# Ten weight splits of a decoder layer's first tile moved behind its softmaxes, and a separate buffer for one gate

## The chip, the cores and the metric

The kernel runs on one core of a Trainium2 chip. The metric is device time in microseconds (us) for one launch. The core's engines are named as in the profile: PE (TensorE matmuls; PEld is its weight load), DVE (VectorE), ACT (ScalarE), POOL (GpSimd) and SP (SyncE, which only issues DMAs here). Each engine works through its own list of instructions in order and waits on semaphores for the others.

## The reference, cut to what matters

One decoder layer over 2048 tokens of width 1024, in float32:

```python
h = rms_norm(x, pre_norm_g)
a_u, a_v, sq, sk, sv, mq, z = split(h @ w_in)          # 512 512 256 128 128 256 1024 columns
y_a = chunked_spatial_gating(gelu(a_u), gelu(a_v))      # chunks of 128 tokens, 4 groups
y_b = sliding_window_attention(sq, sk, sv)              # 4 heads, sinks, relative bias
mk, mv = split(rms_norm(mem, mem_norm_g) @ w_mem_kv)    # 256 memory tokens
y_c = memory_cross_attention(mq, mk, mv)                # 4 heads
y = concat(y_a, y_b, y_c) * silu(z)
x = x + rms_norm(y @ w_out, post_norm_g)
```

## The kernel before, in words

The tokens are worked on in four tiles of 512. For each tile the kernel forms the normalised input `hT` and multiplies it with 22 weight *units*, 128 x 1024 numbers each: four for the values of the spatial gating (`U_V`), then keys, values and queries, then the gate units `U_Z` (z) and the units `U_U` (u). The first tile also projects the memory (`gm`). After the four tiles a second part multiplies y with the output weights.

Precision comes from splitting: each operand is held as a high part (a rounded copy, made by ACT) and a low part (the difference, made by DVE or POOL), and each product is three matmuls: high with high, high with low, low with high. `split` (line 79) does this; the high copy is line 80 and the subtraction is line 81. So a unit is multiplied in 24 matmuls, and its third matmul is the first that reads the unit's low part. A row `whl<-wraw,whl` is the split of one unit from its raw load `wraw` into the pair `whl`.

A unit of the first tile is loaded raw and split once. The pair is then stored to DRAM (`split_d`), and later tiles load it from there. `weight_unit` (line 133) keeps a window: when unit number i of the order is due, units up to i+3 have been split and units up to i+4 are being loaded. There are three raw buffers and four buffers for pairs. Unit i+4's raw load goes into the buffer that held unit i+1's raw, so it waits, on SP, until unit i+1 has been split. SP issues nearly all other DMAs too, in program order: the stores of pairs, the stores `yd` of finished gates, the loads `xs` (for the next tile's sums of squares) and `xk` (the next tile's input).

In the second half of a tile, a counter of *slots* places attention work between the matmuls: one slot after each six matmuls of a unit, and one after each unit. In the first tile twelve softmaxes start in slots 14, 19, 24, 29 (the window attention, names `b_0` to `b_3`) and 33, 36 to 54 (the memory attention, `c_0_0` to `c_3_1`). Each has logits on PE (`l_b`, `l_c`), a maximum on DVE, exponentials on ACT and a normalisation on DVE; its transposes (`tp`) and its product with the values (`o`) follow on PE a fixed number of slots later. The last ten units of the first tile come in this order: U0, Z0, U1, Z1, Z6, Z7, U2, Z2, U3, Z3 (Z0 is `g_z_0` from `whl_10`, U0 is `g_u_0` from `whl_18`, and so on). A unit of kind U ends in a small product `sg` on PE and the tile `a` on DVE.

For later tiles there is a list `aside`: pieces of work put there are taken off one by one by `queue_aside` (line 399), which a softmax calls after its last exponential and its normalisation. They are issued behind these two, ACT work behind the exponential and DVE work behind the normalisation.

The order on PE and SP is the order in which the program is written. On ACT, DVE and POOL the framework's scheduler sets the order when the program is built, within the first part.

Near the end of each tile PE multiplies out `bc` (line 213), the next tile's scale: it needs `rsr_x` from POOL, which needs the sums of squares of eight loads `xs` (line 193 on ACT).

The gates of the window and memory outputs (`ZB`, four per tile, units Z4 to Z7) share two buffers under one tag, so the third gate is written where the first stood, and waits until that one's store to `yd` has landed. Tag `a` has three buffers.

Of the kernel before, what the change touches and what calls it, by code (L numbers as in the profile page):

```python
# [30 lines left out]
U_V, U_SV, U_K, U_Q, U_MQ, U_Z, U_U, U_O, U_MK, U_MV = 0, 4, 5, 6, 8, 10, 18, 22, 30, 32  # L31
# [2 lines left out]

W_OPS = ("B11", "B21", "B22", "T1", "T2", "T3", "T4")
STORE_AFTER = 6
TURN_SLOT = 30
A_SLOTS0, A_SLOTS = (14, 5, 8, 13, 33, 8, 13), (7, 5, 8, 13, 27, 7, 11)

# [2 lines left out]
def kernel(  # L42
# [32 lines left out]

    def f32(ap):
        return ap.bitcast(F32)

    def split(hi, lo, src, lo_engine=None):
        nc.scalar.copy(hi, src)  # L80
        (lo_engine or nc.vector).tensor_tensor(lo, src, f32(hi), ALU.subtract)  # L81
# [22 lines left out]
    made, stores = set(), []  # L104
# [4 lines left out]
    def load_unit(i):  # L109
        u, t = order[i]  # L110
        if u in wo_d or t > stored_at.get(u, 0):
            return
        raws[i] = raw_tile(f"wraw_{t}_{u}")
        for c in (slice(0, 512), slice(512, D)) if i == 0 else (slice(0, D),):
            nc.sync.dma_start(raws[i][:, c], wst[u][:, c])
            yield

    def split_unit(i):
        u, t = order[i]
        w = wp.tile([P, 2, D], F32R, tag="whl", name=f"whl_{t}_{u}")  # L120
        ready[u, t] = w
        if i not in raws:
            nc.sync.dma_start(f32(w), wo_d[u][t] if u in wo_d else split_d[u])
            return
        raw = raws.pop(i)
        for c in (slice(0, 512), slice(512, D)) if i == 0 else (slice(0, D),):
            split(w[:, 0, c], w[:, 1, c], raw[:, c], nc.vector if (i % 3 == 2 and i > 14) or i == 0 else nc.gpsimd)
        if stored_at.get(u) == t:
            stores.append((i, u, w))

    raws, loaded, halved = {}, [0], [0]

    def weight_unit(u, t):

        i = order.index((u, t))
        while halved[0] < min(i + 4, len(order)):
            if loaded[0] == halved[0]:
                list(load_unit(loaded[0]))
                loaded[0] += 1
            split_unit(halved[0])  # L140
            halved[0] += 1
        while loaded[0] < min(i + 5, len(order)):
            list(load_unit(loaded[0]))
            loaded[0] += 1

        while stores and stores[0][0] <= i:
            _, v, w = stores.pop(0)
            nc.sync.dma_start(split_d[v], f32(w))
        return ready.pop((u, t))

    def rms_rstd(ss, n, eps, name, tag=""):
# [86 lines left out]
    def group(w, t, tag, pool=None, slot=None, scaled=True):  # L238

        ps = (pool or ps_mm).tile([P, TS], F32, tag="t" if pool else "mm", name=f"g_{tag}")
        n = 0
        hT = hTs[t % 2]
        for k in range(KC):
            for wi, hi in ((0, 0), (0, 1), (1, 0)):
                nc.tensor.matmul(ps, w[:, wi, k * P : (k + 1) * P], hT[:, hi, k, :],  # L247
                                 start=(n == 0), stop=(n == 3 * KC - 1))
                n += 1
            if slot and k % 2 and k < KC - 1:  # L250
                slot(k // 2)
        if t == 0 and scaled:
            sc = sp.tile([P, TS], F32, tag="a", name=f"sc_{tag}", bufs=3)
            nc.vector.tensor_tensor(sc, ps, late["bcs"], ALU.mult)  # L254
            ps = sc
        return ps
# [87 lines left out]
    def project_memory(mT, slot):  # L344
        for u in range(4):
            w = weight_unit((U_MK if u < 2 else U_MV) + u % 2, 0)
            ps = ps_mm.tile([P, MEM], F32, tag="mm", name=f"gm_{u}")
            n = 0
            for k in range(KC):
                for wi, hi in ((0, 0), (0, 1), (1, 0)):  # L350
                    nc.tensor.matmul(ps, w[:, wi, k * P : (k + 1) * P], mT[:, hi, k, :],  # L351
                                     start=(n == 0), stop=(n == 3 * KC - 1))
                    n += 1
                if k % 4 == 3:
                    slot()
            if u == 3:
                turn_values(2)
            if u < 2:

                mks = sp.tile([P, MEM], F32, tag="e", name=f"mks_{u}", bufs=3)  # L360
                nc.vector.tensor_tensor(mks, ps, late["bcs_mem"], ALU.mult)
                for e in range(2):
                    h = 2 * u + e
                    src = mks[64 * e : 64 * e + 64, :]
                    split(MK[0:64, h, 0, :], MK[0:64, h, 1, :], src)
                    nc.scalar.copy(MK[64:128, h], f32(MK[0:64, h]))
            else:
                mvs = sp.tile([P, MEM], F32, tag="e", name=f"mvs_{u}", bufs=3)
                nc.scalar.copy(mvs, ps)
                late[u] = mvs  # L370

    def turn_values(u):

        tp = ps_mm.tile([P, 2, 2, 64], F32, tag="mm", name=f"mvt_{u}")
        for i in range(2):
            nc.tensor.transpose(tp[:, i].rearrange("p a b -> p (a b)"), late[u][:, i * P : (i + 1) * P], ident)
        hs = slice(2 * (u - 2), 2 * (u - 2) + 2)
        for i in range(2):
            r, hi = late["rstd_mem"][:, i : i + 1], MV[:, i, hs, 0, :]
            nc.scalar.mul(hi, tp[:, i], r)  # L380
            nc.vector.scalar_tensor_tensor(MV[:, i, hs, 1, :], tp[:, i], r, f32(hi), ALU.mult, ALU.subtract)
# [5 lines left out]
    def split_heads(ps, tag, shape_tag):  # L387
        S = sp.tile([P, 2, TS], F32R, tag=shape_tag, name=f"S_{tag}", bufs=1)
        for e in range(2):
            src = ps[64 * e : 64 * e + 64, :]  # L390
            nc.scalar.copy(S[0:64, e, :], src)
            nc.vector.tensor_tensor(S[64:128, e, :], src, f32(S[0:64, e, :]), ALU.subtract)
        return S


    aside = []

    def queue_aside(scalar, vector):
        with tc.issue_after(scalar.ins), tc.issue_after(vector.ins):
# [114 lines left out]
    def silu2(ps, tag, out_tag, bufs):  # L514

        G = sp.tile([P, TS], F32, tag=out_tag, name=f"Z_{tag}", bufs=bufs)
        nc.scalar.activation(G, ps, AF.Tanh, scale=0.5)
        nc.vector.scalar_tensor_tensor(G, G, 1.0, ps, ALU.add, ALU.mult)
        return G
# [3 lines left out]

    def store_later(dst, src, slots=STORE_AFTER):

        stores_due.append((tick[0] + slots, dst, src))
# [88 lines left out]
    for t in range(NT):  # L615
# [44 lines left out]
        for j in range(4):  # L660
# [3 lines left out]
            w = weight_unit(U_V + j, t)  # L664
# [78 lines left out]
        SB, SC, O, ZB = [split_heads(q0, f"q{t}_0", "S0")], [], {}, {}  # L743
# [33 lines left out]
        def slot(_=None):  # L777
            tick[0] += 1
            flush_stores()
            for job in jobs.pop(at[0], []):  # L780
                job()
            for stage, n in sorted(stages.pop(at[0], [])):
                if stage == 2:
                    running[n] = unit(n)
                next(running[n], None)
            if t == 0 and at[0] == TURN_SLOT:
                turn_values(3)
            at[0] += 1

        def slotted(u, tag, scaled=True):  # L790
            ps = group(weight_unit(u, t), t, tag, slot=slot, scaled=scaled)
            return ps
# [8 lines left out]
        def gate_bc(i):  # L801

            ps = slotted(U_Z + 4 + i, f"z{t}_{4 + i}")
            ZB[i] = silu2(ps, f"z{t}_{4 + i}", "ZB", 2)
            slot()

        def gate_a(g):
# [14 lines left out]
            slot()  # L822

        gate_bc(0)
        gate_bc(1)
        if t == 0:
            memory_along()
            project_memory(late["mT"], slot)
        gate_a(0)
        gate_a(1)  # L830
        gate_bc(2)
        gate_bc(3)
        gate_a(2)
# [18 lines left out]

    tick[0] += STORE_AFTER
    T2 = [weight_unit("T2", j) for j in range(2)]
# [327 lines left out]
```

## Time and profile before

| what | value |
|---|---|
| median of 3 runs | 785.67 us (781.81, 785.67, 788.67) |
| the profiled execution's own time | 783.76 us |
| its span, first to last instruction | 781.8 us |
| mean granted TensorE clock | 0.996 |
| busy: PE, PEld | 759.6 us, 638.2 us |
| busy: DVE, ACT, POOL | 567.6 us, 397.4 us, 157.8 us |

The span leaves out 2.0 us of the profiled execution that lie around it. PE is busy nearly all the time, so what a change of the other engines can do is read from the places where PE stands idle, not from the other engines' busy time.

### The profile page before, as it was taken

What the parts mean: (1) busy time and instruction counts of PE and PEld (TensorE: products, weight loads), DVE (VectorE), ACT (ScalarE), POOL (GpSimd) and SP (SyncE); (2) the same over time, 40 slices, a digit from 0 to 9 for tenths busy, and PEclk for the clock granted to TensorE, in tenths of its full rate; (3) what the DMA queues carried; (4) which work ended last, traced back from release to release, by engine and by line L of the source; (5) the groups of instructions that cost most, each with busy time, mean ns of one, the idle gap of its engine ahead of it and who ended that gap; (6) DMA issues with size and microseconds to landing.
All of it is one profiled execution on the core that took longest, in us unless ns stands there. A gap on an engine that the chain in (4) does not pass through costs nothing.

```text
span 781.8 us, 10715 instructions
## 1 busy us (share of the span) xinstructions
PE 759.6 (97%) x3788; PEld 638.2 (82%) x3788; DVE 567.6 (73%) x1052; ACT 397.4 (51%) x879; POOL 157.8 (20%) x141
## 2 busy tenths in 40 slices
PE   8999999899999999999999999999999999999994
PEld 7878987787888888888887788888888878888883
DVE  6497998795658789744796796748976325697787
ACT  7686666653654656355455553544434233343442
POOL 4565543220502210041031000201300000010013
PEclk9999999999999999999999999999999999999998
DMA  8856557736875996947989769864464699818717
GB/s 326 296 205 245 184 204 256 272 123 273 314 261 210 320 316 227 343 165 224 371 292 309 260 218 379 339 261 161 142 216 178 237 388 402 322 55 322 270 32 291
DMA packets 54133, 199.48 MB, mean 255 GB/s; under 512 B 5275, under 2 KB 5824, under 8 KB 43840
## 3 DMA queue, kind: packets, MB, share of 16 engines
q1 hardware_dynamic: 53552, 198.20, 70.1%
q8 instruction: 30, 0.49, 0.2%
q10 hardware_dynamic: 528, 0.59, 0.2%
q14 instruction: 23, 0.19, 0.1%
HBM read 142.15 MB, written 56.63 MB: 254 GB/s over the span
## 4 chain that ended last, share of the span: by engine, by line
PE 70%; DMA 13%; DVE 11%; ACT 3%; issue 2%; POOL 1%; SPq 0%; POOLq 0%; DVEq 0%; ACTq 0%
PE g_z L247 14%; PE v L674 9%; PE g_u L247 7%; PE Y_S L1030 6%; PE Y L1030 5%; PE g_q L247 4%; PE g_mq L247 4%; DMA xs<-in_x 4%; PE X L1030 3%; PE X_S L1030 3%; DMA yd<-Z_z 2%; DMA split_d<-whl 2%; PE g_sv L247 2%; PE g_k L247 2%; PE gm L351 1%
## 5 line engine op out<-in xcount | busy, mean ns | idle before, releaser
L247 PE MATMUL g_z<-hT,whl 128*128 128x512 f32 x768 | 193.7, 396 | 0.0
L247 PEld LDWEIGHTS g_z<-hT,whl 128*128 128x128 f32 x768 | 138.3, 188 | 25.0
L81 POOL TENSOR_TENSOR whl<-wraw,whl 128x1024 fp32r<-128x1024 f32 x30 | 73.6, 2456 | 139.8 <-ACT whl L80 92.8
L247 PE MATMUL g_u<-hT,whl 128*128 128x512 f32 x384 | 97.7, 396 | 0.0
L674 PE MATMUL v<-whl,hT 128*128 128x512 f32 x384 | 88.9, 391 | 2.2 <-DVE sc_z L254 1.7
L674 PEld LDWEIGHTS v<-whl,hT 128*128 128x128 f32 x384 | 71.6, 188 | 18.6 <-DVE sc_z L254 2.1
L247 PEld LDWEIGHTS g_u<-hT,whl 128*128 128x128 f32 x384 | 69.2, 188 | 12.7
L80 ACT CAST whl<-wraw 128x1024 fp32r<-128x1024 f32 (+1 forms) x39 | 40.0, 1027 | 25.5 <-DMA wraw<-in_wst 6.8
L928 POOL TENSOR_TENSOR r<-a,mhalf 128x1 f32<-128x1 f32 x16 | 13.7, 856 | 191.1 <-DVE a L926 178.2
L447 POOL TENSOR_SCALAR_AFFINE_SELECT pp_b<-po_b 128x512 fp32r<-128x512 f32 x30 | 19.9, 663 | 143.3 <-ACT po_b L80 143.3
L247 PE MATMUL g_q<-hT,whl 128*128 128x512 f32 x192 | 45.9, 394 | 0.0
L1030 PE MATMUL Y<-hT,yop 128*128 128x512 f32 x192 | 44.5, 391 | 0.8 <-DVE yop L903 0.8
L247 PE MATMUL g_mq<-hT,whl 128*128 128x512 f32 x192 | 44.7, 389 | 0.0
L1030 PE MATMUL Y_S<-hT,yop_S 128*128 128x512 f32 x192 | 44.2, 389 | 0.0
L1030 PEld LDWEIGHTS Y<-hT,yop 128*128 128x128 f32 x192 | 35.8, 188 | 9.2 <-DVE yop L903 1.7
L1030 PEld LDWEIGHTS Y_S<-hT,yop_S 128*128 128x128 f32 x192 | 36.0, 188 | 7.5
L247 PEld LDWEIGHTS g_q<-hT,whl 128*128 128x128 f32 x192 | 35.7, 188 | 7.8 <-issue 0.5
L247 PEld LDWEIGHTS g_mq<-hT,whl 128*128 128x128 f32 x192 | 35.9, 188 | 7.3
L483 ACT ACTIVATE L_c<-l_c,nm_c 128x256 f32<-128x256 f32 x48 | 22.3, 469 | 28.7 <-DVE nm_c L478 28.6
L432 ACT ACTIVATE Lc_b<-Lc_b,nm_b 128x129 f32<-128x129 f32 x64 | 25.1, 394 | 18.9 <-DVE nm_b L430 18.8
L157 POOL TENSOR_TENSOR rsr_v<-rsa_v,mhalf 128x4 f32<-128x4 f32 x16 | 17.4, 1090 | 82.0 <-DVE rsa_v L155 74.1
L704 ACT ACTIVATE vhat<-G_v,nb,rsr_v 128x128 f32<-128x128 f32 x64 | 26.4, 485 | 11.5 <-DVE nb L702 11.4
(209 smaller groups left out, 1477.2 us busy)
## 6 DMA issues: line engine op xcount, KB each, us to landing
whl<-split_d SPq DMA_DIRECT2D x54, 1024.0 KB, 6.3
split_d<-whl SPq DMA_DIRECT2D x22, 1024.0 KB, 8.3
wraw<-in_wst SPq DMA_DIRECT2D x37, 512.0 KB, 5.8
hT<-wo_B SPq DMA_DIRECT2D x10, 1024.0 KB, 9.3
wo_T<-hT SPq DMA_DIRECT2D x8, 1024.0 KB, 7.8
xr<-in_x SPq DMA_DIRECT2D x16, 512.0 KB, 8.6
y<-yd SPq DMA_DIRECT2D x7, 1024.0 KB, 13.2
xs<-in_x SPq DMA_DIRECT2D x24, 256.0 KB, 6.3
```

Of the source, the lines that this page charges most:

```text
L80: nc.scalar.copy(hi, src)
L81: (lo_engine or nc.vector).tensor_tensor(lo, src, f32(hi), ALU.subtract)
L157: nc.gpsimd.tensor_tensor(r, a, mhalf[:, :c], ALU.pow)
L247: nc.tensor.matmul(ps, w[:, wi, k * P : (k + 1) * P], hT[:, hi, k, :], start=(n == 0), stop=(n == 3 * KC - 1))
L351: nc.tensor.matmul(ps, w[:, wi, k * P : (k + 1) * P], mT[:, hi, k, :], start=(n == 0), stop=(n == 3 * KC - 1))
L432: last = nc.scalar.activation(Lc[:, h, : P + 1], Lc[:, h, : P + 1], AF.Exp, bias=nm[:, h : h + 1], accum_out=den[:, h : h + 1])
L447: nc.gpsimd.affine_select(prev[:, s], f32(own[:, s]), [[0, 4], [-1, P]], ALU.is_gt, 0.0, base=0, channel_multiplier=1)
L483: last = nc.scalar.activation(p[:, e, :], lg[:, e, :], AF.Exp, bias=nm[:, e : e + 1], scale=scale, accum_out=den[:, e : e + 1])
L674: nc.tensor.matmul(vps[i], hT[:, hi, 2 * j + kk, i * P : (i + 1) * P], w[:, wi, kk * 512 : (kk + 1) * 512], start=(j == 0 and (hi, wi, kk) ...
L704: nc.scalar.activation(vhat[:, i, g, :], G[:, g * P : (g + 1) * P], AF.Identity, bias=nb[:, g : g + 1], scale=rv[:, g : g + 1])
L928: nc.gpsimd.tensor_tensor(r, a, mhalf2[:, 0:1], ALU.pow)
L1030: nc.tensor.matmul(banks[m], a(s, k)[:, m * P : (m + 1) * P], w(v, k), start=first and n == 0, stop=n == 11, skip_group_check=not first)
```

## The change

For the first tile, the last ten units (`BEHIND`) are no longer split when the window reaches them. Their split is put on the list `aside`, and the softmaxes of the tile take these pieces off, one each. The raw load, the pair's store and the assertion that a unit is split before it is used stay in their places in the program. Both halves of such a split are on ACT and DVE; before, seven of the ten subtractions were on POOL (those with an order number that isn't 2 modulo 3). In the tiles after the first, the third gate (`i == 2`) takes a buffer of tag `a`; the fourth then stands where the first stood.

```diff
+BEHIND = tuple(range(U_U, U_U + 4)) + (U_Z, U_Z + 1, U_Z + 2, U_Z + 3, U_Z + 6, U_Z + 7)
...
         raw = raws.pop(i)
+        if t == 0 and u in BEHIND:
+
+            aside.append([lambda: split(w[:, 0], w[:, 1], raw), lambda: pending.discard(u)])
+            pending.add(u)
+            stores.append((i, u, w))
+            return
         for c in (slice(0, 512), slice(512, D)) if i == 0 else (slice(0, D),):
             split(w[:, 0, c], w[:, 1, c], raw[:, c], nc.vector if (i % 3 == 2 and i > 14) or i == 0 else nc.gpsimd)
...
+        assert u not in pending
         return ready.pop((u, t))
...
         def gate_bc(i):
 
             ps = slotted(U_Z + 4 + i, f"z{t}_{4 + i}")
-            ZB[i] = silu2(ps, f"z{t}_{4 + i}", "ZB", 2)
+
+            ZB[i] = silu2(ps, f"z{t}_{4 + i}", *(("a", 3) if i == 2 and t else ("ZB", 2)))
             slot()
```

The instructions on PE and on SP stand in the same order as before. On POOL seven subtractions are gone. ACT and DVE are ordered anew by the scheduler. Line numbers in the changed kernel are 5 to 12 higher.

DVE around the start of Z0, in the kernel before. `sc_u_0` to `a_0` close U0; `nm_b_3`, `den_b_3` and `Lc_b_3` belong to the fourth softmax; `whl_16` is unit Z6:

```order
L254 TENSOR_TENSOR sc_u_0_1111<-g_u_0_1052,bcs_486 128x512
L430 TENSOR_REDUCE nm_b_3_1066<-Lc_b_3_1065 128x4
L814 SCALAR_TENSOR_TENSOR a_0_1124<-sg_0_1119,g_v,addend 128x512
L81 TENSOR_TENSOR whl_16_1127<-wraw_16_1049,whl_16_1127 128x1024
L381 SCALAR_TENSOR_TENSOR MV<-mvt_1098,rsr_mem,MV 128x2x64
L508 SCALAR_TENSOR_TENSOR e_u_0_1113<-e_u_0_1113,sc_u_0_1111 128x512
L434 RECIPROCAL den_b_3_1067<-den_b_3_1067 128x4
```

DVE at the same place in the changed kernel:

```order
L440 TENSOR_REDUCE nm_b_3_1060<-Lc_b_3_1059 128x4
L393 SCALAR_TENSOR_TENSOR MV<-mvt_1094,rsr_mem,MV 128x2x64
L266 TENSOR_TENSOR sc_u_0_1107<-g_u_0_1046,bcs_486 128x512
L825 SCALAR_TENSOR_TENSOR a_0_1120<-sg_0_1115,g_v,addend 128x512
L444 RECIPROCAL den_b_3_1061<-den_b_3_1061 128x4
L445 TENSOR_TENSOR Lc_b_3_1059<-Lc_b_3_1059,den_b_3_1061 128x4x128
L86 TENSOR_TENSOR whl_10_924<-wraw_10_881,whl_10_924 128x1024
```

The split of Z0's own unit (`whl_10`) now stands here, behind `a_0`, which reads `sg_0`, the last product on PE ahead of Z0; before, it stood ahead of the third softmax, and a unit needed three units later stood here.

DVE ahead of U1 (`whl_19`), in the changed kernel; `nm_c_0_0` to `L_c_0_0` are the first memory softmax, and `sc_z_0` reads Z0's finished product. In the kernel before, `whl_19` was not on DVE:

```order
L488 TENSOR_REDUCE nm_c_0_0_1172<-l_c_0_0_1166 128x2
L490 TENSOR_TENSOR nm_c_0_0_1172<-nm_c_0_0_1172,rsr_x_260 128x2
L495 RECIPROCAL den_c_0_0_1173<-den_c_0_0_1173 128x2
L496 TENSOR_TENSOR L_c_0_0_1171<-L_c_0_0_1171,den_c_0_0_1173 128x512
L266 TENSOR_TENSOR sc_z_0_1194<-g_z_0_1127,bcs_486 128x512
L86 TENSOR_TENSOR whl_19_983<-wraw_19_925,whl_19_983 128x1024
```

U1's low part is now made after Z0, the unit straight ahead of U1, has ended.

ACT ahead of the last squares `xs_3_0` and `xs_3_1`, in the kernel before; `L_c_3_0` and `L_c_3_1` are the last two softmaxes, `e_u_2` is unit U2:

```order
L483 ACTIVATE L_c_3_0_1549,den_c_3_0_1551<-l_c_3_0_1544,nm_c_3_0_1550,rsr_x_260 128x256 x2
L193 ACTIVATE xs_3_0_1571,ss_1_1320<-xs_3_0_1571 128x512
L499 COPY oh_c_1_0_1579<-o_c_1_0_1574 64x256
L193 ACTIVATE xs_3_1_1602,ss_1_1320<-xs_3_1_1602 128x512
L80 CAST pT_c_2_0_1593<-tp_c_2_0_1588 128x512
L483 ACTIVATE L_c_3_1_1615,den_c_3_1_1617<-l_c_3_1_1610,nm_c_3_1_1616,rsr_x_260 128x256 x2
```

ACT at the end of the same stretch in the changed kernel:

```order
L509 COPY oh_c_1_1_1651<-o_c_1_1_1646 64x256
L517 ACTIVATE e_u_2_1632<-sc_u_2_1630 128x512
L493 ACTIVATE L_c_3_1_1613,den_c_3_1_1615<-l_c_3_1_1608,nm_c_3_1_1614,rsr_x_260 128x256 x2
L85 CAST whl_13_1558<-wraw_13_1468 128x1024
L85 CAST pT_c_2_1_1672<-tp_c_2_1_1667 128x512
L85 CAST whl_0_1654<-wraw_0_1559 128x1024
L519 ACTIVATE e_u_2_1632<-e_u_2_1632 128x512
L205 ACTIVATE xs_3_0_1569,ss_1_1316<-xs_3_0_1569 128x512
L205 ACTIVATE xs_3_1_1600,ss_1_1316<-xs_3_1_1600 128x512
```

The last squares have moved from ahead of the last softmax to behind it, and behind two casts and U2's two activations.

More of the change, by code (lines that the diff above doesn't have):

```diff
@@ L77, in f32 @@
         return ap.bitcast(F32)
+    aside = []
     def split(hi, lo, src, lo_engine=None):
@@ L129, in split_unit @@
             stores.append((i, u, w))
-    raws, loaded, halved = {}, [0], [0]
+    raws, loaded, halved, pending = {}, [0], [0], set()
     def weight_unit(u, t):
@@ L393, in split_heads @@
         return S
-    aside = []
     def queue_aside(scalar, vector):
```

## The prediction

> **What bounds the kernel now.** First the page: its span and its line of busy times; beside them one row of the chain of waits, an undisturbed unit of 24 matmuls (start, length, what).
>
> ```profile
> span 781.8 us, 10715 instructions
> PE 759.6 (97%) x3788; PEld 638.2 (82%) x3788; DVE 567.6 (73%) x1052; ACT 397.4 (51%) x879; POOL 157.8 (20%) x141
> 35.32 5.44 PE g_k L247 x24
> ```
>
> PE is the bound: 22 us of the span are not PE's, and most of those lie before the first and after the last product. A unit takes 5.44 us, 0.227 per matmul, and the change leaves every matmul as it is. So only PE's idle time can move. Next, then, the waits of PE over the whole span (total, times, longest):
>
> ```profile
> PE o_c L497 <- DVE OC L501: 1.7, 2, 1.4
> PE l_c L473 <- DVE nm_c L480: 1.7, 1, 1.7
> PE v L674 <- DVE sc_z L254: 1.7, 1, 1.7
> PE o_c L497 <- DVE pT_c L81: 1.5, 1, 1.5
> PE tp_c L491 <- DVE pT_c L81: 1.2, 1, 1.2
> PE o_b L457 <- POOL po_b L449: 0.4, 1, 0.4
> PE sg L812 <- ACT L_c L483: 0.3, 1, 0.3
> ```
>
> By the same view cut by tiles, rows one to three and the last two lie in the second half of the first tile, or at the first product of the second: 5.8 us. Rows four and five are in the third tile: 2.7 us. The second and fourth tiles have none. So all that this change could win is 8.5 us, 1.1% of the time; what it can lose is open.
>
> **What the seven POOL subtractions cost.** The timeline of POOL and DVE in the first tile (start, length):
>
> ```profile
> 90.73 5.19 POOL L81 TENSOR_TENSOR whl<-wraw,whl 128x1024 fp32r<-128x1024 f32 x2 [5.22 <-ACT whl L80]
> 91.15 5.05 DVE L429 TENSOR_TENSOR Lc_b<-L_b 128x256 f32<-128x256 f32 x2
> 102.67 0.41 DVE L429 TENSOR_TENSOR Lc_b<-L_b 128x256 f32<-128x256 f32 x1
> 121.59 1.99 DVE L508 SCALAR_TENSOR_TENSOR e_u<-e_u,sc_u 128x512 f32<-128x512 f32 x1 [1.13 <-ACT e_u L507]
> 135.34 2.54 DVE L486 TENSOR_TENSOR L_c<-L_c,den_c 128x512 f32<-128x512 f32 x1
> 138.74 0.14 DVE L480 TENSOR_TENSOR nm_c<-nm_c,rsr_x 128x2 f32<-128x2 f32 x1
> 147.65 1.49 DVE L480 TENSOR_TENSOR nm_c<-nm_c,rsr_x 128x2 f32<-128x2 f32 x1
> 98.86 0.69 DVE L435 TENSOR_TENSOR Lc_b<-Lc_b,den_b 128x512 f32<-128x512 f32 x1
> ```
>
> While POOL subtracts, a DVE instruction with both inputs in SBUF stands: two of 0.41 took 5.05, one of about 0.69 took 1.99 and another 2.54, one of 0.14 took 1.49. Excess: 4.2 + 1.3 + 1.85 + 1.35 = 8.7 us over the seven. What the change puts on DVE instead, from the groups of the stretch 78 to 182 us:
>
> ```profile
> L81 POOL TENSOR_TENSOR whl<-wraw,whl 128x1024 fp32r<-128x1024 f32 x10 | 25.4, 2540 | 47.8 <-ACT whl L80 47.8
> L81 DVE TENSOR_TENSOR whl<-wraw,whl 128x1024 fp32r<-128x1024 f32 x4 | 4.9, 1215 | 0.0
> ```
>
> Seven more subtractions of 1.22: 8.5 us. For DVE's time this is a wash, 0.2 us to the good; POOL, which PE waits for but once (0.4), is 7 x 2.54 = 18 us lighter. [...]
>
> **What the moved splits cost.** A split now stands behind a softmax, close ahead of its unit. The PE and DVE rows at the first three units:
>
> ```profile
> 86.48 1.12 PE L422 MATMUL l_b<-KK,S_q 128*128 128x256 f32 x8
> 92.81 3.02 PE L247 MATMUL g_u<-hT,whl 128*128 128x512 f32 x12
> 99.62 1.05 PE L812 MATMUL sg<-wsp,vhat 128*128 128x128 f32 x8
> 100.43 1.62 PE L247 MATMUL g_z<-hT,whl 128*128 128x512 f32 x6
> 108.02 1.52 PE L247 MATMUL g_u<-hT,whl 128*128 128x512 f32 x6
> 87.81 1.22 DVE L81 TENSOR_TENSOR whl<-wraw,whl 128x1024 fp32r<-128x1024 f32 x1
> 88.94 1.40 DVE L428 SCALAR_TENSOR_TENSOR L_b<-l_b,rstd_q,bias 128x512 f32<-128x512 f32 x2
> 96.12 0.16 DVE L416 COPY Lc_b<-sink_bc 128x4 f32<-128x4 f32 x1
> 98.65 0.18 DVE L434 RECIPROCAL den_b<-den_b 128x4 f32<-128x4 f32 x1 [0.97 <-ACT Lc_b L432]
> 104.46 0.73 DVE L814 SCALAR_TENSOR_TENSOR a<-sg,g_v,addend 128x512 f32<-128x512 f32 x1
> 112.01 0.68 DVE L254 TENSOR_TENSOR sc_z<-g_z,bcs 128x512 f32<-128x512 f32 x1
> ```
>
> A unit's first two matmuls need only the high part, so PE stands 2 x 0.227 = 0.45 us less than the subtraction is late.
>
> *U0*, behind the third softmax (its logits are the row at 86.48). Its first DVE step starts at 87.81 instead of 88.94, since the subtraction there is gone. To the two L429 it is 91.15 - 88.94 = 2.2: 90.0. These take 0.8 without POOL: 90.8. From the copy (96.12) to the reciprocal (98.65), maximum and exponentials included, 2.5: 93.3. Reciprocal and normalisation 0.8, subtraction 1.2: 95.3. PE wants the low part at 92.81 + 0.45: **2.0 us** (1 to 3.5; ACT's cast is done inside it).
>
> *Z0*. On DVE its subtraction is behind `a_0`, which waits for `sg`, straight ahead of Z0 on PE (99.62, over at 100.43). From there 0.73 + 0.18 + 0.69 + 1.22 = 2.8, less 0.45: **2.3 us** (2 to 3.5). It cannot be nothing while DVE's order is this one.
>
> *U1*. Its subtraction is behind `sc_z_0`, which waits for Z0's end, where U1 would start: 0.68 + 1.22 - 0.45 = **1.5 us** (1.4 to 2.5).
>
> From Z1 on the softmax is four to ten slots ahead of the unit, 6 us of PE or more, and its chain is about 4.5 (the 2.8 above with a maximum and two exponentials): nothing, but a DVE backlog of 2 us would show. Sum: 5.8 us.
>
> *The scale `bc`.* ACT's last squares now stand behind U2's activation. Rows for that chain, PE first:
>
> ```profile
> 148.65 1.54 PE L247 MATMUL g_u<-hT,whl 128*128 128x512 f32 x6
> 157.11 1.05 PE L213 MATMUL bc<-ident,rsr_x 128*128 128x128 f32 x8
> 154.29 0.56 ACT L483 ACTIVATE L_c<-l_c,nm_c,rsr_x 128x256 f32<-128x256 f32 x1 [1.61 <-DVE Lc_b L416]
> 155.39 1.04 ACT L80 CAST whl<-wraw 128x1024 fp32r<-128x1024 f32 x1
> 152.54 1.01 POOL L157 TENSOR_TENSOR rsr_x<-rsa_x,mhalf 128x4 f32<-128x4 f32 x1 [3.42 <-DVE rsa_x L155]
> 127.76 0.63 ACT L193 ACTIVATE xs<-xs 128x512 f32<-128x512 f32 x1 [2.42 <-DMA xs<-in_x]
> L193 ACT ACTIVATE xs<-xs 128x512 f32<-128x512 f32 x8 | 5.0, 628 | 7.2 <-DMA xs<-in_x 7.2
> ```
>
> U2 ends at 148.65 + 6 x 0.227 = 150.0, and `bc` starts 7.1 later, 0.6 of it the small waits above: 6.5 us of PE work. In the changed order there lie between the same two points: `sc_u_2` 0.68; on ACT the activation 0.63, two exponentials 1.1 (154.29 to 155.39), a cast 1.04, a short one 0.6, a cast 1.04, an activation 0.63, two squares with their accumulator reads some 1.4; on DVE about 1.0 (two small steps around one of 0.69); on POOL 1.01. Sum 9.1, so `bc` is 2.6 late at the least. To this I add 1.8: DVE has the split of U3 ahead of `sc_u_2` (1.2), and the squares wait for their loads (7.2 / 8 = 0.9 each in the row), of which a part shows. These loads are behind SP: unit i+4's raw load waits there for the split of unit i+1, now late, and the `yd` stores, pair stores and `xs` loads queue behind it. I take **4.5 us** (2 to 9).
>
> *What goes.* The wait for `OC` (1.4 of 1.7) came from the L486 row stretched by POOL; the one for `nm_c` from DVE standing behind ACT, which stood for `xs` (the row at 127.76), and these squares move back; the one for `sc_z` at the second tile's first product from DVE's backlog, and PE's new waits of 10 us give DVE that time. I count all 5.8 us as gone (down to 2).
>
> *The third gate.* One ACT row of the third tile:
>
> ```profile
> 442.41 0.60 ACT L517 ACTIVATE Z_z<-g_z 128x512 f32<-128x512 f32 x1 [3.51 <-DMA yd<-Z_z]
> ```
>
> ACT stood 3.5 us for the first gate's store, and the transposed probabilities behind it were late for `tp_c`: that 1.2 us goes (0 to 1.2). The 1.5 beside it stays; what stood there was again an `xs` load.
>
> **Sum:** + 5.8 + 4.5 - 5.8 - 1.2 = + 3.3 us. Against the profiled execution's own 783.76 that is 787.1. The median of the runs shown, 785.67, is 1.9 above it, which would give 789.0. I say 788.
>
> **The rivals.**
>
> *Only the early waits come.* `xs` loads land early, DVE keeps up, `bc` is on time: + 5.8 - 7.0 = - 1.2, so 782.6 to 784.5. For it: ACT is busy half the time. Against: the order of ACT's list. 22%.
>
> *The cover holds everywhere.* No new wait, and all the old ones go: - 7.0, 776.8 to 778.7. It needs Z0's subtraction not to be behind `a_0`, which DVE's order excludes, or a faster DVE. 8%.
>
> *SP's queue decides (slower).* With raw loads held on SP until the late splits, the last `xs` loads leave late; ACT stands for each (0.9 mean, 2.4 at the worst in this tile before) with casts and probabilities queued behind it, and `bc` is 9 late; of the old waits on DVE only half go. 5.8 + 9 - 3.5 = + 11.3: 795.1 to 797.0. It decides from a `bc` wait of about 8 on. For it: 7.2 us of ACT's idle time in this stretch is already this load. 17%.
>
> *DVE becomes the bound of this half.* [...] As a mechanism here: the 8.5 us land on DVE, the 8.7 come back at places where it was idle anyway, and its backlog at the tile's end makes PE wait 8 us longer: 791.8 to 793.7. Against: the 8.7 us stood inside softmaxes. 10%.
>
> My forecast (785 to 791) has 40%; 3% is for what I don't see.
>
> **Range and chances.** What a measurement of this kernel can tell from no change is about 1%: 777.8 to 793.5. Faster by more than that: half of the second rival and a little, 5%. Slower by more: the SP rival and the upper part of the last, 18%. Within: 77%. The range 780 to 796 leaves out the second rival, half of the SP one and the 3%.
>
> **What would show it.** PE waits at `g_u`, `g_z`, `g_u` in the first tile for DVE `whl`, of 2.0, 2.3 and 1.5; one at `bc` for POOL `rsr_x` of 2 to 9; no wait for `OC` or `sc_z`; every L429 near 0.41; POOL's busy time near 140; no 3.5 us for `yd<-Z_z` in the third tile, and no `tp_c` wait. The forecast is wrong if the three early waits are missing, if `bc` has none, or if PE waits for `whl` from Z1 on.

## The result, and the profile after

The changed kernel takes 791.85 us (median, 791.5 to 792.27), the kernel before beside it 786.73 (781.81 to 788.67): the ratio is 1.0088, with a 95% interval of 1.0064 to 1.0113. That is 5.1 us more on the medians (0.65%, at the low end of that interval). The profiled executions, 783.76 before and 791.5 after, are 7.7 apart, and their spans 7.8.

In the changed kernel L86 is the subtraction that was L81, and L259 the products that were L247. The page, span and busy times:

```profile
span 789.6 us, 10710 instructions
PE 763.9 (97%) x3788; PEld 642.2 (81%) x3788; DVE 565.5 (72%) x1059; ACT 397.2 (50%) x879; POOL 139.2 (18%) x134
```

PE has the same 3788 matmuls and is busy 4.3 us longer: some of them ran more slowly. DVE has the seven subtractions more and is busy 2.1 us less, POOL 18.6 less. PE's waits in the second half of the first tile (total, times, longest):

```profile
PE bc L225 <- POOL rsr_x L169: 5.7, 1, 5.7
PE g_u L259 <- ACT whl L85: 1.6, 2, 0.9
PE g_u L259 <- DVE whl L86: 1.5, 2, 1.0
PE g_z L259 <- ACT whl L85: 1.1, 1, 1.1
PE g_z L259 <- DVE whl L86: 0.9, 1, 0.9
```

These five stand where before there were `OC`, `nm_c`, `sc_z`, `po_b` and `L_c`; all of those are gone. Now PE's timeline at two of the waits (start, length, instruction; in brackets what it waited for), and the same stretches cut into windows of 3.41 us (the columns are busy time and count of PE, PEld, DVE, ACT and POOL, then the granted clock):

```profile
103.97 0.73 PE L259 MATMUL g_z<-hT,whl 128*128 128x512 f32 x2 [1.15 <-ACT whl L85]
105.61 1.63 PE L259 MATMUL g_z<-hT,whl 128*128 128x512 f32 x4 [0.90 <-DVE whl L86]
...
166.43 2.08 PE L225 MATMUL bc<-ident,rsr_x 128*128 128x128 f32 x8 [5.71 <-POOL rsr_x L169]
168.16 1.20 PE L507 MATMUL o_c<-pT_c,MV 128*128 128x256 f32 x4
169.16 2.40 PE L259 MATMUL g_z<-hT,whl 128*128 128x512 f32 x6
```

```profile
92.50:95.91 3.41, 2.01 (x12) 1.30 (x11) 2.60 (x5) 3.34 (x9) 0.22 (x1) 1.00 0.00 0
...
102.74:106.15 3.41, 1.36 (x5) 0.78 (x5) 3.25 (x6) 1.97 (x5) 0.00 (x0) 1.00 0.00 0
106.15:109.57 3.42, 3.42 (x16) 3.19 (x14) 1.65 (x3) 1.16 (x2) 0.00 (x0) 0.50 0.84 240
...
112.98:116.39 3.41, 2.11 (x9) 1.10 (x7) 2.20 (x4) 2.71 (x6) 0.54 (x1) 1.00 0.00 0
...
160.76:164.18 3.42, 0.00 (x0) 0.00 (x0) 3.42 (x5) 2.22 (x6) 0.00 (x0) 1.00 1.02 392
164.18:167.59 3.41, 1.16 (x5) 1.16 (x6) 1.11 (x4) 0.00 (x0) 1.01 (x1) 0.50 0.94 270
167.59:171.00 3.41, 3.41 (x14) 3.02 (x13) 2.06 (x4) 0.99 (x2) 0.00 (x0) 0.50 0.86 356
171.00:174.42 3.42, 3.42 (x19) 2.82 (x18) 2.81 (x5) 2.69 (x4) 1.70 (x1) 1.00 0.32 95
```

Behind Z0's waits and behind `bc` the granted clock is 0.50, and six matmuls of a gate take 2.40 us instead of 1.55. In these three windows PE was busy 3.42 + 1.16 + 3.41 = 8.0 us at half the clock, so 4.0 us of it are lost. In the trace of before the clock is halved nowhere until 776 us, behind PE's last product.

Where the 7.8 us arise: `g_sv`, the first product behind the four units `U_V` of the second tile, starts at 197.85 before and here at

```profile
207.39 4.92 PE L259 MATMUL g_sv<-hT,whl 128*128 128x512 f32 x21
```

that is 9.5 later (where a tile is said to begin sooner or later below, it is by the start of its `g_sv`); 0.25 of it was there before the stretch. The sum of the first tile is + 5.2 (the three units) + 5.7 (`bc`) + 4.0 (the clock) - 5.8 (the old waits) = + 9.1. The second tile adds 0.8 (a new wait of 0.9 for `o_c`), the third gives 2.5 back (no wait for `tp_c`, 0.8 at `o_c` instead of 1.5). From there on the two run alike.

### The profile page after: what moved, and what is told of

It is laid out like the page before. It is cut to its first block, busy times and chain, and to the rows that moved or that the text cites. A ratio compares the mean times of both kernels' runs of the same rounds, so it can differ in the third digit from the quotient of the medians.

```text
span 789.6 us, 10710 instructions
## 1 busy us (share of the span) xinstructions
PE 763.9 (97%) x3788; PEld 642.2 (81%) x3788; DVE 565.5 (72%) x1059; ACT 397.2 (50%) x879; POOL 139.2 (18%) x134
## 4 chain that ended last, share of the span: by engine, by line
PE 74%; DVE 11%; DMA 9%; ACT 3%; issue 2%; SPq 0%; POOLq 0%; POOL 0%; DVEq 0%; ACTq 0%
PE g_z L259 15%; PE v L684 11%; PE g_u L259 8%; PE g_q L259 6%; PE g_mq L259 6%; PE Y L1041 5%; DMA xs<-in_x 5%; PE Y_S L1041 4%; PE g_sv L259 3%; PE g_k L259 3%; PE X_S L1041 3%; PE X L1041 2%; DMA yd<-Z_z 2%; PE o_c L507 2%; PE tp_c L501 1%
## 5 line engine op out<-in xcount | busy, mean ns | idle before, releaser
L259 PE MATMUL g_z<-hT,whl 128*128 128x512 f32 x768 | 195.3, 398 | 2.1 <-ACT whl L85 1.1
L259 PEld LDWEIGHTS g_z<-hT,whl 128*128 128x128 f32 x768 | 139.2, 190 | 27.9 <-DVE whl L86 1.3
L259 PE MATMUL g_u<-hT,whl 128*128 128x512 f32 x384 | 98.3, 397 | 3.1 <-ACT whl L85 1.6
L259 PEld LDWEIGHTS g_u<-hT,whl 128*128 128x128 f32 x384 | 68.9, 188 | 17.0 <-DVE whl L86 2.4
L86 POOL TENSOR_TENSOR whl<-wraw,whl 128x1024 fp32r<-128x1024 f32 x23 | 55.5, 2417 | 104.9 <-ACT whl L85 104.8
L939 POOL TENSOR_TENSOR r<-a,mhalf 128x1 f32<-128x1 f32 x16 | 13.7, 858 | 191.1 <-DVE a L937 178.1
L259 PE MATMUL g_q<-hT,whl 128*128 128x512 f32 x192 | 45.9, 394 | 0.0
L259 PE MATMUL g_mq<-hT,whl 128*128 128x512 f32 x192 | 44.7, 389 | 0.0
L259 PEld LDWEIGHTS g_q<-hT,whl 128*128 128x128 f32 x192 | 35.8, 188 | 7.8 <-issue 0.5
L259 PEld LDWEIGHTS g_mq<-hT,whl 128*128 128x128 f32 x192 | 35.9, 188 | 7.3
L914 DVE TENSOR_TENSOR yop<-y,yop 128x1024 fp32r<-128x1024 f32 x12 | 14.6, 1219 | 24.0 <-ACT yop L908 24.0
```

What stands on the lines that cost most here:

```text
L914: nc.vector.tensor_tensor(w[:, 1, ks], yraw[name, p][:, ks], f32(w[:, 0, ks]), ALU.subtract)
L939: nc.gpsimd.tensor_tensor(r, a, mhalf2[:, 0:1], ALU.pow)
```

## The experiments

Ratios are to the kernel before, timed beside each on the same chip; 0.001 of it is 0.8 us.

### Each part alone

The gate without the splits is one line put into the kernel before:

```diff
-            ZB[i] = silu2(ps, f"z{t}_{4 + i}", "ZB", 2)
+            ZB[i] = silu2(ps, f"z{t}_{4 + i}", *(("a", 3) if i == 2 and t else ("ZB", 2)))
```

> The kernel before with the third gate's new place alone, no split moved. Theory (the places are separate, and the gate was worth the waits of the third tile): the wait for tp_c (1.2 us) is gone and that for o_c in the third tile falls from 1.5 to about 0.8, so 1.2 to 2.0 us faster than before; the first tile's waits (OC, nm_c, sc_z) stay at about 1.7 each. Rival (those waits went because the weights' splits moved the whole schedule, or the gate takes a buffer from the products a): no faster than before, within 0.5 us, or a new wait of DVE for a.

0.9976 (0.9952 to 1.0001), so 1.9 us faster, and not told apart from nothing. In its trace the third tile has no wait of PE over 0.2 us at all; the second has got one for `o_c`, 1.2. The splits without the gate are the reverse of that line in the changed kernel:

> The changed kernel with the third gate back at its old place. Theory: the splits alone cost what the first tile lost, 9 us on the span by the stages of the two traces, with the waits 1.4, 2.1 and 1.7 at the first three units and 5 to 6 at bc; about 8 to 10 us slower than before by the span, and tp_c waits 1 to 1.5 again. Rival (the gate is worth nothing): as the changed kernel, 5 to 8 us slower, and no wait for tp_c.

1.0086 (1.0056 to 1.0116), the time of the whole change within the intervals, and its span 789.5 the same. The three early waits (1.8 + 1.5 + 2.0) and `bc` (5.7) are all there, in the third tile 1.4 at `o_c`. The 1.3 at `tp_c` that was expected again is there, but in the second tile, not in the third. So the gate's worth is missing in this comparison. The two traces show what hides it: here the same 2.0 us at Z0 did not halve the clock, since they fell across the border of two windows (1.08 us of standing in the one, 0.98 in the next), and the second tile begins 1.7 us sooner than in the changed kernel (205.73 against 207.39). Over the second and third tiles 1.5 of this is lost again: the fourth begins at 501.59 against 501.73.

### Is it the clock?

Matmuls that compute nothing that is used are put into the waits:

```diff
+        for _ in range({"u0_0": 6, "z0_0": 9, "u0_1": 8}.get(tag, 0)):
+            nc.tensor.matmul(ps, hT[:, 0, 0, 0:P], hT[:, 0, 1, :], start=True, stop=True)
...
         bc = ps_t.tile([P, TS], F32, tag="t", name=f"bc_{t}")
+        for _ in range(25 if t == 1 else 0):
+            nc.tensor.matmul(bc, hTs[0][:, 0, 0, 0:P], hTs[0][:, 0, 1, :], start=True, stop=True)
```

> The changed kernel with matmuls on data that lies ready, written where the next product overwrites them, ahead of the three units and of bc: 6, 9, 8 and 25 of 0.227 us, which is 1.4, 2.0, 1.8 and 5.7 us, the lengths of the waits. They compute nothing that is used. Theory (the slow matmuls behind Z0's start and behind bc come from the clock, which was halved because TensorE had stood): the granted clock is 1.00 in both places, six matmuls of a gate take 1.55 us there instead of 2.40, and the kernel is 3 to 4 us faster than the changed one, though PE does 48 matmuls more. Rival (the matmuls there are slow for another reason, contention for their operands or the chip's power): the rates stay, and the time is that of the changed kernel within 1 us.

Timeline of PE, and the clock at Z0 and around `bc`:

```profile
164.38 1.05 PE L227 MATMUL bc<-ident,rsr_x 128*128 128x128 f32 x8
165.19 0.72 PE L511 MATMUL o_c<-pT_c,MV 128*128 128x256 f32 x4
165.74 1.55 PE L263 MATMUL g_z<-hT,whl 128*128 128x512 f32 x6
```

```profile
102.41:107.78 5.37, 5.09 (x30) 4.13 (x29) 4.40 (x9) 2.86 (x8) 0.00 (x0) 1.00 0.23 53
...
163.00:166.00 3.00, 3.00 (x21) 2.71 (x20) 0.53 (x1) 0.00 (x0) 0.90 (x1) 1.00 0.77 242
```

The same matmuls, with the same operands at the same place, take 1.05 instead of 2.08, 0.72 instead of 1.20 and 1.55 instead of 2.40. Only PE's standing was taken away, so the half clock comes from that. The second tile begins 4.2 us sooner than in the changed kernel (4.0 were worked out above). The whole is 1.0059 (1.0033 to 1.0084), 2.3 us less than the changed kernel by the ratios, under the 3 to 4 that were expected: later on its trace waits 1.3 and 1.5 us for `o_c` and 1.2 in the second part, where the changed kernel has 0.9, 0.8 and nothing.

How long must PE stand? The kernel before, with ten round trips from PE to DVE and back, of growing length:

```diff
+        def pause(n):
+            pz = ps_t.tile([P, P], F32, tag="t", name=f"pz_{t}_{n}")
+            nc.tensor.matmul(pz, turn, ident, start=True, stop=True)
+            for _ in range(n):
+                nc.vector.tensor_copy(turn, ident)
+            nc.tensor.matmul(pz, turn, ident, start=True, stop=True)
```

> The kernel before with ten pauses of TensorE of growing length in the second and third tiles, each a matmul that waits for a chain of 2 to 40 small copies on VectorE which itself waits for a matmul ahead; nothing of it is used. Theory (a halved clock follows a wait that is long enough, or several short ones close together): behind single pauses below about 2 us the clock stays at 1.00, behind those above 3 to 4 us it is 0.5 for 3 to 6 us, which costs 1.5 to 3 us more than the wait. Rival (the dips in the first tile come from the work there): the clock is 1.00 behind every pause.

Windows of its trace, around the pause of 0.6 us and the next one, of 5.0:

```profile
224.38:227.79 3.41, 2.83 (x15) 2.26 (x14) 0.77 (x3) 0.00 (x0) 0.00 (x0) 1.00 0.49 202
...
241.45:244.86 3.41, 1.31 (x7) 0.94 (x5) 2.67 (x7) 1.91 (x9) 0.94 (x1) 1.00 0.86 298
244.86:248.28 3.42, 0.53 (x3) 0.53 (x3) 2.76 (x7) 0.00 (x0) 1.82 (x3) 0.50 0.02 10
248.28:251.69 3.41, 3.41 (x12) 2.83 (x11) 0.00 (x0) 0.00 (x0) 0.04 (x1) 0.50 0.00 0
251.69:255.10 3.41, 3.41 (x19) 2.92 (x18) 2.68 (x6) 0.39 (x2) 0.00 (x0) 1.00 0.00 0
```

The pause began at 242.8 and ended at 247.8; the clock fell at 244.86 and came back at 251.69, 3.9 us behind the pause. All nine stretches at half clock in the second and third tiles of this run, a single execution, are 6.8, 10.2, 13.7 or 17.1 us long, where 3 to 6 behind the wait were expected; that is two to five times 3.41, and their borders all lie on one grid of 3.41 us. So it isn't the wait's length that counts but how much of one window PE stood: with 0.6 idle nothing, with 2.1 of 3.4 the next window is halved, and the window in which PE starts again (here from 248.28 on, busy for all its 3.41 us) is paid too. What the pauses don't bracket, waits of 1 to 2 us, the other traces do: below.

### What makes `bc` late?

The next tile's squares four slots earlier in the first tile, all else as changed:

```diff
-            ... if t else (n_slots - 28, n_slots - 10, 1)
+            ... if t else (n_slots - 32, n_slots - 10, 1)
```

> The changed kernel with the next tile's squares four slots earlier in the first tile, so that the last two stand ahead of U2's activation on ACT, not behind two casts. Theory (bc waits for ACT's list, in which casts stand ahead of the last squares): bc's wait falls from 5.7 to under 1.5 us, and the granted clock behind it stays at 1.00; 6 to 8 us less than the changed kernel, so between 1.5 us faster and 2 us slower than before. Rival one (bc waits for the loads behind SP, or for DVE with U3's subtraction ahead): the wait stays at 3 us or more. Rival two (what is taken from bc comes back as waits for probabilities, since squares now stand ahead of pT_c): the bc wait goes, but PE waits for o_c or tp_c for 3 us or more in the first tile.

PE's waits, first at `bc`, then the longest in the second tile, where there are two more of 0.9 and 0.8:

```profile
PE bc L225 <- POOL rsr_x L169: 1.1, 1, 1.1
```

```profile
PE o_c L507 <- DVE pT_c L86: 2.0, 1, 2.0
```

The wait falls from 5.7 to 1.1, with the clock at 1.00 behind it: the second tile begins 6.4 us sooner than in the changed kernel. So the place of the squares in ACT's list, behind U2's activation, made `bc` late. Two other parts are not separated by this run: it moves the squares' loads with them, and the scheduler moved U3's subtraction too, which no longer stands right ahead of `sc_u_2`. The loads can be little of it, since ACT stood only 1.0 us for all eight of them in the changed kernel. What was behind it shows in the changed kernel's ACT and DVE, shortly ahead of `bc`:

```profile
160.18 1.05 ACT L85 CAST whl<-wraw 128x1024 fp32r<-128x1024 f32 x1
...
162.27 0.62 ACT L205 ACTIVATE xs<-xs 128x512 f32<-128x512 f32 x1
```

```profile
162.67 1.21 DVE L86 TENSOR_TENSOR whl<-wraw,whl 128x1024 fp32r<-128x1024 f32 x1
...
164.40 0.15 DVE L208 TENSOR_TENSOR ss<-ss 128x4 f32<-128x4 f32 x1
```

The last squares stand behind casts, and their sum (L208) behind another subtraction. The run as a whole is 1.0017 (0.9991 to 1.0044), 5.6 us less than the changed kernel, just short of what was expected: 3.7 us of the gain are given back in the second tile. The wait for `o_c` of 2.0 fell into one window, which left PE 1.42 us busy in it, and cost another half window:

```profile
285.47:288.88 3.41, 1.42 (x8) 0.89 (x7) 1.43 (x3) 2.36 (x5) 0.00 (x0) 1.00 0.91 345
288.88:292.30 3.42, 3.42 (x13) 2.84 (x12) 3.38 (x9) 1.81 (x7) 0.00 (x0) 0.50 0.24 98
```

### Engine or place?

The change does two things to the ten splits: it takes seven subtractions from GpSimd, and it puts all ten behind softmaxes. Three runs fill the table, all with the gate's new place. The later seven units alone behind their softmaxes:

```diff
-BEHIND = tuple(range(U_U, U_U + 4)) + (U_Z, U_Z + 1, U_Z + 2, U_Z + 3, U_Z + 6, U_Z + 7)
+BEHIND = (U_U + 2, U_U + 3, U_Z + 1, U_Z + 2, U_Z + 3, U_Z + 6, U_Z + 7)
```

> The changed kernel with the first three units (U0, Z0, U1) split as before, at once, and only the other seven behind their softmaxes. Theory (the early waits come from the softmax being close ahead of the unit, from Z1 on it is far enough): no wait for whl anywhere, no clock dip behind Z0; the last squares stand ahead of U2's activation on ACT here, so bc waits under 2 us. 10 to 13 us less than the changed kernel, 2 to 5 us faster than before. Rival (DVE's added time is what costs, wherever the splits stand): the three waits move to other products (OC, sc_z, l_c), 3 us or more in the first tile, and the kernel is not faster than before.

0.9912 (0.9876 to 0.9948): 6.9 us faster than before, where 2 to 5 were expected, and 14 less than the changed kernel. No wait for `whl`, none at `bc`; 1.1 at `sc_z`, 1.1 at `l_c` and 0.7 at `tp_c`, 2.9 in all. The kernel before with VectorE for all ten, in their old place:

```diff
-            split(w[:, 0, c], w[:, 1, c], raw[:, c], nc.vector if (i % 3 == 2 and i > 14) or i == 0 else nc.gpsimd)
+            split(w[:, 0, c], w[:, 1, c], raw[:, c], nc.vector if i > 15 or i == 0 else nc.gpsimd)
```

> The kernel before with the third gate's new place and with VectorE doing all ten subtractions, each where it stood before, at once, not behind a softmax. Theory (the engine is not what costs, the place is): no wait for whl, the stretched rows of DVE (two L429 in 5.05 us) are gone, bc waits under 2 us, and the kernel is 2 to 6 us faster than before. Rival (seven subtractions of 1.22 us more on DVE delay what PE waits for): the old waits for OC, nm_c, sc_z grow from 1.7 to 2.5 or more each, and the kernel is 2 us or more slower than before.

0.9876 (0.9835 to 0.9917), 775.79 us: the fastest of all, and 9.7 us faster than before, where 2 to 6 were expected. But the edit reaches further than the ten. Not every unit is split only once, as the words on the kernel before have it: the four units `U_V` are split again in the second tile, and the four behind them in the second and the third. `i > 15` holds for these splits too, so GpSimd has fifteen subtractions fewer, seven of the ten and eight others. The group on both pages, before and in this run:

```profile
L81 POOL TENSOR_TENSOR whl<-wraw,whl 128x1024 fp32r<-128x1024 f32 x30 | 73.6, 2456 | 139.8 <-ACT whl L80 92.8
```

```profile
L81 POOL TENSOR_TENSOR whl<-wraw,whl 128x1024 fp32r<-128x1024 f32 x15 | 36.2, 2419 | 21.0 <-ACT whl L80 20.9
```

The traces tell how much the eight can matter. Against the run with the gate alone, the first `g_sv` product of the second tile starts 8.0 us sooner (190.43 against 198.46), and the spans are 7.7 apart, so six of the eight, which lie at that point or behind it, show no gain. The other two, for the next tile's units, lie ahead of it: in the kernel before GpSimd makes them from 161.19 to 164.03 and from 172.82 to 175.79, and under them DVE had

```profile
162.62 2.62 DVE L227 SCALAR_TENSOR_TENSOR xk<-xk,colt,bcs 128x512 f32<-128x512 f32 x2
174.12 2.22 DVE L508 SCALAR_TENSOR_TENSOR e_u<-e_u,sc_u 128x512 f32<-128x512 f32 x1
```

where 1.5 and 0.7 are usual. Behind these rows stands `sc_z`, for which PE waited 1.9 us in the gate's run; that part of the gain may be theirs, and isn't separated. Now 78 to 182 us of the kernel before, then of this one:

```profile
78.00:182.00 104.00, 98.24 (x572) 84.80 (x572) 92.15 (x153) 64.03 (x146) 34.58 (x23) 1.00 0.62 215
```

```profile
78.00:182.00 104.00, 104.00 (x604) 91.12 (x604) 94.52 (x167) 65.65 (x148) 11.88 (x14) 1.00 0.63 219
90.91 0.76 DVE L429 TENSOR_TENSOR Lc_b<-L_b 128x256 f32<-128x256 f32 x2
```

PE does 604 matmuls here instead of 572 and stands for nothing, with DVE busy in 94.5 of the 104 us. The pair of L429 that took 5.05 us takes 0.76. The fourth field of the table, the changed kernel with seven subtractions given back to GpSimd:

```diff
-            aside.append([lambda: split(w[:, 0], w[:, 1], raw), lambda: pending.discard(u)])
+            aside.append([lambda: split(w[:, 0], w[:, 1], raw, nc.vector if i % 3 == 2 else nc.gpsimd), lambda: pending.discard(u)])
```

> The changed kernel, the ten splits behind their softmaxes, but seven of the ten subtractions on GpSimd as before (U0 and U1 of the first three among them). Theory (a unit waits for its subtraction, 2.54 us on GpSimd instead of 1.22): the waits at U0 and U1 grow by about 1.3 each to 2.7 and 3.0, Z0's stays or grows, as DVE's instructions with two inputs in SBUF stand still under GpSimd's again; bc waits 4 to 7. 3 to 8 us slower than the changed kernel. Rival (the place alone sets the waits, the engine is idle anyway): the same three waits within 0.4 us, and the time of the changed kernel within 1.5 us.

1.0107 (1.007 to 1.0145). U0 and U1 wait 1.7 each for the subtraction now, which makes 2.6 with the cast; `bc` waits longer still:

```profile
PE bc L225 <- POOL rsr_x L169: 8.0, 1, 8.0
PE g_u L259 <- POOL whl L86: 3.4, 2, 1.7
PE g_u L259 <- ACT whl L85: 1.7, 2, 0.9
```

By the ratios that is 1.5 us more than the changed kernel, where 3 to 8 were expected. DVE's instructions stand still under POOL's here too, as was expected, only other ones. The pairs of L439 take 0.75, but under POOL's subtractions from 136.32 to 138.86 and from 160.96 to 163.31 there are

```profile
137.44 1.97 DVE L528 SCALAR_TENSOR_TENSOR Z_z<-Z_z,sc_z 128x512 f32<-128x512 f32 x1
161.75 2.10 DVE L768 SCALAR_TENSOR_TENSOR Z_z<-OC,Z_z 128x512 f32<-128x512 f32 x1
```

which take about 0.7 elsewhere. The table of ratios:

| | at once, in place | behind softmaxes |
|---|---|---|
| seven on GpSimd | 0.9976 | 1.0107 |
| all ten on VectorE | 0.9876 (again: 0.9907), with eight others | 1.0088 (the change) |

The place costs 10 us with GpSimd. The lower row, 14 to 17 us apart, isn't like with like, as its left field has eight subtractions more on VectorE. But the run with the later seven leaves these eight on GpSimd, gives only the first three units their old place back (two of them with GpSimd), and is 14 us less than the changed kernel; so most of it is the place. The engine wins 5 to 8 us in place, of which the `sc_z` part, up to 1.9, may belong to the other two; behind the softmaxes its 1.5 us are not told apart from nothing.

### Which units, and once more

Beside a repeat of the fastest one, its two halves: the first three units behind their softmaxes and the rest in place on VectorE, and the reverse. Both edits also have the line `i > 15` from above, so the eight other subtractions are on VectorE in all of them.

```diff
+BEHIND = (U_U, U_Z, U_U + 1)
```

> As the run with all ten subtractions on VectorE in place and the third gate's new place, but the first three units (U0, Z0, U1) split behind their softmaxes as in the changed kernel; the other seven at once, on VectorE. Theory (the early waits are those three units' alone, and bc was late only because all ten stood behind softmaxes): waits for whl of 1.4, 2.0 and 1.7, and a halved clock for 3.4 us if 2 us of them fall into one window of 3.4 us; bc waits under 1.5; so 5 to 7 us more than the run with all ten in place, 3 to 5 us faster than before. Rival (the three splits drag the loads on SP with them, and bc's wait with them): bc waits 4 to 6 us, and the kernel is 2 us or more slower than before.

1.0045 (1.0028 to 1.0063): 11 us more than with all ten in place, where 5 to 7 were expected, and so slower than before by 3.5 instead of faster by 3 to 5. `bc` has no wait. The waits at the three units, and ACT at Z0:

```profile
PE g_z L259 <- ACT whl L85: 4.0, 1, 4.0
PE g_u L259 <- ACT whl L85: 1.8, 2, 0.9
PE g_u L259 <- DVE whl L86: 1.5, 2, 1.0
```

```profile
103.05 0.37 ACT L392 ACTIVATE MV<-mvt,rsr_mem 128x128 fp32r<-128x128 f32 x1 [1.96 <-DVE MV L393]
```

Z0 waits 4.0 for its cast (ACT starts it at 105.80) instead of 1.1 + 0.9, since ACT stood 2.0 for DVE, which had another unit's subtraction ahead; a half window follows (106.8 to 110.2). The sum is 7.3 of waits at the units + 1.7 of clock + 0.9 at `sc_z` = 9.9 of 11. The reverse:

```diff
+BEHIND = (U_U + 2, U_U + 3, U_Z + 1, U_Z + 2, U_Z + 3, U_Z + 6, U_Z + 7)
```

> As the run with all ten subtractions on VectorE in place, but the later seven units (Z1 on) split behind their softmaxes; the first three at once, on VectorE. Theory (from Z1 on the softmax is far enough ahead, and the place costs or wins nothing): no wait for whl, the time of the run with all ten in place within 2 us, about 9 to 11 us faster than before. Rival one (behind the softmax the splits leave DVE free for what PE waits for): 2 us or more faster than with all ten in place. Rival two (they delay the probabilities behind them): waits for tp_c, o_c or sc_z, and 2 to 5 us slower than with all ten in place.

0.9918 (0.989 to 0.9947), 776.58 us against 776.12 with all in place: from Z1 on the place is free, and wins nothing. (It is 6.4 us faster than before, where 9 to 11 were expected.) Neither half has a wait at `bc`; only all ten together have it. What in the scheduler's planning puts the squares behind the casts then wasn't settled.

> The kernel before with all ten subtractions on VectorE in place, and nothing else: the third gate stays where it was. Theory (gate and subtractions are separate): 1.5 to 2.5 us more than the same kernel with the gate's new place, the difference in the third tile (tp_c 1.2, o_c 0.7 more), so 7.5 to 9 us faster than before. Rival (the gate's new place is what won in the third and fourth stretch of that run): 4 us or more of difference.

The fastest kernel with the gate in its old place: 0.9913 (0.9887 to 0.994), 776.56 us, 0.4 us from its pair and 6.8 faster than before, where 7.5 to 9 were expected. The gate's worth, expected at 1.5 to 2.5, is not shown by the three comparisons: 1.9 alone, about nothing in the two others.

> The run with all ten subtractions on VectorE in place and the third gate's new place once more, on the chip of its three variants. Theory: 10 us faster than before again (8 to 12), with no wait of PE for an engine in the first tile. Rival (it was a lucky placing of PE's waits in the windows of the clock): 5 us or less.

0.9907 (0.9878 to 0.9935), 7 us faster than before: under the 8 that were expected, but the gain stands. The profiled execution was the longest of its seven, 781.27 against 775.28 for the shortest, and its trace tells why. In the second and third tiles PE waited for `o_c`, 2.1 and 2.5 us; of the first the window and the one behind it:

```profile
275.47:278.88 3.41, 1.35 (x9) 1.21 (x9) 2.04 (x5) 2.36 (x5) 0.00 (x0) 1.00 0.97 329
278.88:282.29 3.41, 3.41 (x12) 2.83 (x11) 3.41 (x9) 2.67 (x9) 0.00 (x0) 0.50 0.90 291
```

The earlier profile of this kernel had one wait of 1.2 there and no half window. The waits are 3.4 us more, two half windows 3.4: 6.8 of the 7.1 us between the two spans. So here the wait of 2.1 us, with 2.06 of standing in one window, cost 2.1 + 1.7 = 3.8, and no half clock followed the 2.0 at Z0 that fell across two windows in the run with the splits alone (1.08 and 0.98).

## Why the prediction was right, and where it was wrong

The time came within the range: 3.9 us above the forecast, and slower, as its likeliest case had it, by 0.9% instead of 0.4. It lies above that case's own 785 to 791, among the figures of the rival with DVE as the bound (791.8 to 793.7), whose mechanism did not come. So that the number came within the range is owed to its width, and what speaks for the prediction is its steps: the waits came where it named them. One by one, against the profiled execution:

- **The early waits: right.** U0 waited 0.87 + 0.53 = 1.4 (2.0 forecast), Z0 2.05 (2.3), U1 0.75 + 0.99 = 1.74 (1.5): 5.2 instead of 5.8. All three include ACT's cast, which the prediction had inside the chain. From Z1 on there was none, as forecast, and the run with the later seven alone shows that this place is free.
- **`bc`: right in kind, low in size.** 5.7 instead of 4.5. The reason given first, the order of ACT's list, is what the earlier squares took away. The waits for `xs`, part of the 1.8 added, were hardly a part of it: in that stretch they fell from 7.2 to 1.0 us (the group of squares on ACT, and the idle time ahead of them):

```profile
L205 ACT ACTIVATE xs<-xs 128x512 f32<-128x512 f32 x8 | 5.0, 627 | 1.0 <-DMA xs<-in_x 1.0
```

What the sum hadn't was DVE's subtraction for the next tile's first unit, ahead of L208.
- **What failed: a price for the wait alone.** The sum put every wait at its length. The clock behind Z0 and `bc` added 4.0 us, which the run with the waits filled confirms (4.2). This is the largest missing term: the sum came 4.4 short, of which 4.0 is the clock, 1.2 `bc`, - 0.6 the early waits, 0.8 the second tile's new `o_c` wait, - 1.3 the third tile, 0.25 ahead of it all.
- **What goes: right in size, one reason open.** All 5.8 us went. Whether the `sc_z` wait needed PE's new waits to give DVE time isn't shown: with the ten in place on VectorE it goes as well, but that run also takes from GpSimd the two subtractions that stretched DVE's rows ahead of `sc_z`. Where these two stay, in the first run with the later seven behind softmaxes, 1.1 of it is left.
- **DVE's time: the wash was a sum over the wrong thing.** 8.7 freed against 8.5 added was near enough. DVE is 2.1 us less busy, so 10.6 were freed; among the rows that the 8.7 left out is `nm_c` at 113.44, which took 1.01 instead of 0.14 under GpSimd's subtraction from 112.05 on. Yet the in-place run, with fifteen subtractions more on DVE and its busy time 2.6 us up, is 7 to 10 us faster than before. What GpSimd stretched were in part instructions that PE waited for; what was added made PE wait nowhere in the first tile.
- **The third gate: 1.2 forecast, 2.5 gained in the third tile, 0.8 lost in the second.** The `tp_c` wait is gone, as said; the `o_c` wait was to stay and halved. Alone it is 1.9 us, with an interval that ends just above nothing.
- **The rivals.** SP's queue needed a `bc` wait of 8: it was 5.7. DVE as the bound is refuted by the in-place run, which has more work on DVE and no wait of PE in the first tile. The times of the case in which the cover holds everywhere, 776.8 to 778.7, are about what VectorE brought with the ten (and the eight) where they stood: 775.79 and 776.12.

## What to carry to other kernels

A change that moves work to another engine and to another place at once is two changes: here the engine won 5 to 8 us, and the place lost 10 to 14. Count on the page what an edit moved: a condition meant for ten splits reached eight others. Ask for each moved piece how much of TensorE's work lies between its new place and its use: with 6 us or more (the prediction's count), from Z1 on, it was free, and straight ahead of the unit, at the first three, it was late. Price a wait of TensorE of about 2 us or more with the half clock that can follow it (here it did behind 1.99 us of standing in one window), 1.7 us for each busy window of 3.41.

## What the runs showed of the hardware

In the traces here the granted clock changes on a grid of 3.41 us, fixed within a run: the stretches at 0.50, other than the one at the end, are one or more whole windows (from 3.41 at 106.15 in the changed kernel to 17.1 in the run with the pauses), none a part of one. Which window was halved went by how much of the one ahead PE stood. With 1.30, 1.40 and 1.30 us idle (the kernel before at 178.74, the changed one at 92.50 and 112.98) the next one is full, and so it is with 1.68, the largest in the kernel before ahead of its end:

```profile
127.54:130.95 3.41, 1.73 (x10) 1.24 (x9) 1.92 (x5) 3.16 (x7) 0.00 (x0) 1.00 0.88 365
130.95:134.37 3.42, 3.42 (x21) 2.91 (x20) 3.42 (x7) 3.31 (x9) 0.00 (x0) 1.00 0.44 168
```

With 1.99 (the earlier squares), 2.05 (the changed kernel at Z0), 2.06 (the repeat) and 2.10 (the pauses) it is halved. So in these runs the border lies between 1.68 and 1.99 us of 3.41, and several short waits add up: Z0's were 1.15 and 0.90 with matmuls between them. In the changed kernel the clock is back at 1.00 behind the halved windows that PE filled (3.42 us busy from 106.15 on, 3.41 from 167.59 on), and stays at 0.50 behind the one with 1.16 us busy (from 164.18 on).
